# A two-layer LRU, attention and pooling trunk: the scheduler's order of the engine queues taken from its other simulated machine

## The chip, the cores and the metric

One core of a Trainium2 chip runs the kernel. The metric is the device time of one execution in microseconds, the median of the runs shown; less is better.

## The reference

The model has two layers over 2048 rows of 1024 features, and a final norm. Every layer makes 18 column groups of `z` from the normed input, runs three branches on them and projects their gated results back:

```python
for l in range(DEPTH):
    h = rms_norm(x, norm_g[l])
    z = h @ w_in[l]
    za, ga, cq, ckv, kr, gb, zc, gc = jnp.split(z, offsets, axis=-1)
    xa = causal_depthwise_conv(za, conv_w[l], conv_b[l])
    ya = rg_lru(xa, w_rg[l], b_rg[l], w_ig[l], b_ig[l], lru_lambda[l]) * jax.nn.silu(ga)
    yb = mla(cq, ckv, kr, q_norm_g[l], w_uq[l], kv_norm_g[l], w_ukv[l], cos, sin) * jax.nn.silu(gb)
    yc = multi_scale_pool(zc, w_pool[l], pool_scale[l]) * jax.nn.silu(gc)
    y = jnp.concatenate([ya, yb, yc], axis=-1)
    x = x + y @ w_out[l]
return rms_norm(x, final_norm_g)
```

`mla` norms the latents `cq` (384 wide) and `ckv` (256 wide), makes six heads of queries, keys and values from them, and runs causal attention with a rotary part of 32 in every head.

## The kernel before, in words

Data lie transposed: features on the 128 partitions, rows of the sequence along the free dimension, in four chunks of 512. Every matmul operand is split into a high and a low fp16 half, so that a product takes three passes (high by high, high by low, low by high).

**A layer, stage by stage.** `hstage` loads the eight k-tiles of a chunk (L303), multiplies them by the reciprocal norm (L334, alternately on GpSimd, POOL, and on VectorE, DVE), and writes the high half `hA` or `hB` on ScalarE, ACT (L336), and the low half on DVE (L337). `zweight` and `prep` do the same for weights: load (L216), squares on ACT (L222), their sum by a small matmul `pp` on TensorE, PE (L228), a power-of-two scale on DVE (L185 to L190), the halves (L231 on ACT, L232 on DVE). `zgroup` makes one column group of one chunk from 24 matmuls (L378). What follows a group, such as the LRU (L448 to L486), the pooling or the latents (`latent`, L561 to L583, whose column sums of squares are the `pn` matmuls of L245 behind the halves of L238 and L239), runs on ACT and DVE. `values_of` (L719) makes values, copied to `zw` by ACT (L727) and DVE (L728); `keys` is L708, `query` L736, `q_rope` L750. For a softmax without a running maximum, each unit of four query blocks and two heads first has its row maxima taken (`row_max`: matmuls `pm` L777 with two PSUM banks, maxima L782 and L784 on DVE, a transposing matmul L802, and L806 on ACT into a row of `kq`).

**Attention** runs over 12 units (four chunks by three pairs of heads) and over their blocks of 128 keys: scores (L980 to L984), exponentials on ACT (L985), the low half on DVE (L986), the weighted values (L999, L1004). `finish` divides (L949 to L955), transposes (L961), gates to `y` (L963) and stores it (L400).

**Output projection.** `outproj` loads the eight rows of `y` of a chunk (L1023), scales and splits them to `yb` (L1018 and the scale, L1026 on ACT, L1027 on DVE), multiplies them by the output weights (L1046, 24 matmuls per n), adds the load of the old `x` (L1053, L1054), stores the new `x` (L1055) and sums its squares (L1060, L1061) for the next norm. The last chunk of the last layer goes through `outproj_last` (L1073 to L1111). At the end of layer 1, `layer_start` of layer 2 is started beside the last chunk's projection: its `hstage` for chunks 0 and 1 and its first six weights.

**What sets the order.** All of these are Python generators. `spawn` starts one, `tick` advances those that are due, and `between` fills in pieces between matmuls. So the program has one written order. The tile layer then orders each engine's queue itself: it simulates the instructions on a model of the machine and issues what the model finds ready. Loads and stores are all issued from SyncE's queue (SP). Tiles come from pools with fixed numbers of buffers: `T` has 7, `LT` 17; PSUM has three banks under "mm", two under "ax", and one each under "sm", "po" and "su". An engine's queue runs in the order given; an instruction that waits holds up those behind it.

The context that holds this scheduler is opened in `launch`, at L1325:

Of the kernel before, what the change touches and what calls it, by code (L numbers as in the profile page):

```python
# [1316 lines left out]
def launch(nc, ins, outs):  # L1317
    from contextlib import ExitStack

    a = {}  # L1320
    for k, v in ins.items():
        a[k] = nc.dram_tensor(k, v.shape, F32, kind="ExternalInput").ap()
    for k, s in outs.items():
        a[k] = nc.dram_tensor(k, s, F32, kind="ExternalOutput").ap()
    with tile.TileContext(nc) as tc, ExitStack() as ctx:  # L1325
        body(nc, tc, a, ctx)
    if not nc.is_finalized():
        nc.finalize()
# [9 lines left out]
```

## Time and profile before

| what | value |
|---|---|
| median of 3 runs | 2011.38 us |
| lowest and highest run | 2005.93 and 2012.34 us |
| profiled execution | 2005.98 us |
| its span in the trace | 2004.2 us |
| mean granted TensorE clock, as a share of full speed | 0.982 |
| PE busy | 1897.2 us, 95% |
| DVE busy | 1553.8 us, 78% |
| ACT busy | 1159.9 us, 58% |
| POOL busy | 100.7 us, 5% |
| PE instructions in the trace (weight loads apart) | 12524 |

A span is the time from the first to the last instruction in the trace; the execution's own time has 1.8 us more around it. Engine rows overlap, so busy times don't add up to the span. A line number names the line of the kernel that issued an instruction, and `out<-in` its tiles. In the windows and the timeline, times count from the start of the span. A bracket at a row's end gives the idle time of the engine before the row and the instruction that ended it.

### The profile page before, as it was taken

How to read it: one execution, taken by the hardware profiler on the slowest of the kernel's cores; microseconds unless marked ns; L12 is line 12 of the kernel's file. 1: busy time of each engine (PE TensorE's matmuls, PEld its weight loads, DVE VectorE, ACT ScalarE, POOL GpSimd, SP SyncE). 2: the span in 40 equal slices, each digit the busy share in tenths (PEclk: the TensorE clock that was granted, in tenths of full speed). 3: DMA queues.
4: the chain of work that ended last, by engine and by line, in shares of the span. 5: the costliest groups of instructions: out<-in, count | busy, mean ns of one | idle time of the engine just before them, and what ended most of it. 6: DMA issues, size and time to landing. Idle time of an engine off the chain costs nothing. (4 is left out here: it accounts for less than half of the span.)

```text
span 2004.2 us, 33235 instructions
## 1 busy us (share of the span) xinstructions
PE 1897.2 (95%) x12524; PEld 993.1 (50%) x12524; DVE 1553.8 (78%) x3438; ACT 1159.9 (58%) x2042; POOL 100.7 (5%) x70
## 2 busy tenths in 40 slices
PE   7889999899999999999889999999999999999997
PEld 3334444444455555555344444444445555555556
DVE  7987788767788788785868568777587977978756
ACT  7677877644455464464446678775444644545533
POOL 1210000011000000000211000001010000000000
PEclk8999999999999999999899999999999999999999
DMA  5221222203453131122742113212134522322353
GB/s 181 91 73 57 90 74 93 80 28 79 99 172 118 44 91 43 43 70 60 244 146 85 48 58 99 87 61 87 48 83 119 189 64 69 112 64 69 117 163 132
DMA packets 117553, 186.94 MB, mean 93 GB/s; under 512 B 13072, under 2 KB 45968, under 8 KB 117392
## 3 DMA queue, kind: packets, MB, share of 16 engines
q1 hardware_dynamic: 117392, 184.82, 30.0%
q8 instruction: 98, 1.61, 0.4%
q14 instruction: 63, 0.52, 0.1%
HBM read 113.99 MB, written 55.05 MB: 84 GB/s over the span
## 5 line engine op out<-in xcount | busy, mean ns | idle before, releaser
L378 PEld LDWEIGHTS <-zw 128*128 128x128 f16 x3456 | 336.8, 100 | 419.9 <-issue 41.7
L985 ACT ACTIVATE p<-sps,tiny,sig 128x512 f32<-128x512 f32 x480 | 321.3, 710 | 320.8 <-PE sps L982 178.1
L378 PE MATMUL zps<-hA,zw 128*128 128x512 f16 x1728 | 392.3, 384 | 8.0 <-ACT hA L336 4.8
L378 PE MATMUL zps<-hB,zw 128*128 128x512 f16 x1728 | 384.1, 379 | 5.1 <-DVE hB L337 3.3
L1046 PE MATMUL ops<-yb,wo 128*128 128x512 f16 x1344 | 338.0, 384 | 10.8 <-DVE yb L1027 5.7
L986 DVE TENSOR_TENSOR pl<-p 128x1024 f16<-128x1024 f32 x240 | 254.2, 1060 | 102.9 <-ACT p L985 79.0
L782 DVE TENSOR_REDUCE mx<-pm 128x1 f32<-128x512 f32 x288 | 193.0, 683 | 29.7 <-PE pm L777 29.1
L1046 PEld LDWEIGHTS <-wo 128*128 128x128 f16 x1344 | 127.3, 98 | 153.1 <-issue 25.6
L980 PE MATMUL sps<-kq 97*128 97x512 f16 x480 | 167.1, 348 | 0.6 <-ACT p L985 0.6
L981 PE MATMUL sps<-kq 96*128 96x512 f16 x480 | 166.7, 347 | 0.0
L982 PE MATMUL sps<-kq 96*128 96x512 f16 x480 | 165.7, 345 | 0.0
L777 PE MATMUL pm<-kq 96*128 96x512 f16 (+2 forms) x480 | 146.8, 347 | 3.6 <-ACT kq L806 1.4
L999 PE MATMUL av<-zw,p 128*128 128x129 f16 (+1 forms) x1632 | 140.6, 216 | 5.9 <-DVE o L953 5.8
L999 PEld LDWEIGHTS <-p 128*128 128x128 bf16 x1632 | 108.5, 98 | 35.4 <-DVE o L953 5.9
L784 DVE CUSTOM_DVE_ANT_0 pm<-pm,mkq 128x128 f32<-128x128 f32 x192 | 93.2, 494 | 9.8 <-PE pm L777 9.2
L999 PE MATMUL av<-zw,pl 128*128 128x65 f16 x1632 | 94.7, 195 | 1.5 <-DVE pl L986 1.4
L222 ACT ACTIVATE junk<-raw 128x512 bf16<-128x512 f32 (+3 forms) x126 | 75.1, 596 | 16.7 <-DMA raw<-win 13.4
L999 PEld LDWEIGHTS <-pl 128*128 128x128 f16 x1632 | 76.4, 98 | 10.1 <-DVE pl L986 5.4
L334 POOL TENSOR_TENSOR xk<-xk,rb 128x512 f32<-128x512 f32 x28 | 46.2, 1682 | 602.7 <-DVE of L1042 458.4
L982 PEld LDWEIGHTS <-kq 96*128 96x128 f16 x480 | 46.9, 98 | 45.1 <-issue 1.7
L980 PEld LDWEIGHTS <-kq 97*128 97x128 f16 x480 | 46.6, 97 | 44.2 <-issue 4.5
L981 PEld LDWEIGHTS <-kq 96*128 96x128 f16 x480 | 47.2, 98 | 42.3 <-issue 4.1
(301 smaller groups left out, 2848.6 us busy)
## 6 DMA issues: line engine op xcount, KB each, us to landing
raw<-win SPq DMA_DIRECT2D x72, 256.0 KB, 3.5
yr<-y SPq DMA_DIRECT2D x64, 256.0 KB, 4.2
x<-xr SPq DMA_DIRECT2D x56, 256.0 KB, 2.5
xk<-x SPq DMA_DIRECT2D x56, 256.0 KB, 4.8
sg<-sg SPq DMA_DIRECT2D x48, 256.0 KB, 3.6
kq<-pq SPq DMA_DIRECT2D x96, 128.0 KB, 2.4
raw<-wout SPq DMA_DIRECT2D x32, 256.0 KB, 3.6
wo<-wp SPq DMA_DIRECT2D x32, 256.0 KB, 2.7
```

The source lines that it names most:

```text
L222: nc.scalar.activation(junk[:, 0 : kp * n], raw[:, 0 : kp * n], AF.Square, accum_out=ssq[:, i : i + 1])
L378: nc.tensor.matmul(ps[:], w[:, i, k, :], st["h"](j, k, c), start=n == 0, stop=n == 3 * KD - 1)
L777: nc.tensor.matmul(pm[:, 0:n], t[0:96, h, 2, q0 : q0 + 128], t[0:96, h, 0, s * C : s * C + n], start=True, stop=True)
L782: nc.vector.tensor_reduce(m, pm[:], AX.X, ALU.max)
L784: nc.vector.tensor_tensor_reduce(out=pm[:, 0:n], in0=pm[:, 0:n], in1=mkq[:, C - n : C], op0=ALU.add, op1=ALU.max, scale=1.0, scalar=-3.0e3 ...
L980: nc.tensor.matmul(ps[:, o:C], t[0:97, h, 0, ks], t[0:97, h, 2, qs], start=True, stop=False)
L981: nc.tensor.matmul(ps[:, o:C], t[0:96, h, 0, ks], t[0:96, h, 3, qs], start=False, stop=False)
L982: nc.tensor.matmul(ps[:, o:C], t[0:96, h, 1, ks], t[0:96, h, 2, qs], start=False, stop=not diag)
L985: nc.scalar.activation(pw_[:, h, o:C], ps[:, o:C], AF.Exp, scale=sig[:, 4:5], bias=tiny[:, 1:2])
L986: nc.vector.tensor_tensor(pl[:, :, o:C], pw_[:, :, o:C], ph[:, :, o:C], ALU.subtract)
L999: nc.tensor.matmul(acc[h][:, c - 64 * lo : c + 65], w, v[:, 64 - 64 * lo : QB], start=first and n == 0 and j == 0, stop=end and n == 1 and ...
L1046: nc.tensor.matmul(ps[:], w[:, i, k, :], yb[:, j, k, :], start=m == 0, stop=m == 3 * KD - 1)
```

## The change

The context is opened with one more argument. It makes the tile layer's scheduler run the other of its two simulated machines, and the queues are ordered by what that one finds ready:

```diff
@@ -1322,7 +1322,7 @@
         a[k] = nc.dram_tensor(k, v.shape, F32, kind="ExternalInput").ap()
     for k, s in outs.items():
         a[k] = nc.dram_tensor(k, s, F32, kind="ExternalOutput").ap()
-    with tile.TileContext(nc) as tc, ExitStack() as ctx:
+    with tile.TileContext(nc, schedule_with_timeline_sim=True) as tc, ExitStack() as ctx:
         body(nc, tc, a, ctx)
     if not nc.is_finalized():
         nc.finalize()
```

The instructions stay the same: 12446 matmuls by the program's count, 801 DMAs, and every ACT and DVE operation. What moves is their place in the queue of their engine: 8894 of PE's 12451 places hold another instruction than before, 2788 of DVE's, 1174 of ACT's, 304 of SP's; POOL's order is the same. Semaphore waits are set anew for the new order.

**First place: ACT at the start.** `raw` are loaded weights, `lsa` squares of the first chunk, `zw_72` the weights' halves, and `hA` the halves of the first normed chunk. Before:

```order
L319 ACTIVATE lsa<-lsa 128x512 x2
L222 ACTIVATE junk,ssq<-raw 128x512 x2
L231 ACTIVATE zw_72<-raw,zsc 128x512 x2
L222 ACTIVATE junk,ssq<-raw 128x512 x2
L319 ACTIVATE lsa<-lsa 128x512
L231 ACTIVATE zw_72<-raw,zsc 128x512
L336 ACTIVATE hA<-xk,gs 128x512 x7
```

Now:

```order
L319 ACTIVATE lsa<-lsa 128x512 x4
L222 ACTIVATE junk,ssq<-raw 128x512 x3
L231 ACTIVATE zw_72<-raw,zsc 128x512 x2
L222 ACTIVATE junk,ssq<-raw 128x512
L231 ACTIVATE zw_72<-raw,zsc 128x512 x2
L222 ACTIVATE junk,ssq<-raw 128x512 x3
L132 ACTIVATE sp<-sp 128x6
L133 ACTIVATE sp<-sp 128x6
L222 ACTIVATE junk,ssq<-raw 128x512
L336 ACTIVATE hA<-xk,gs 128x512 x3
```

More squares and halves of weights, and the two small gate rows, stand ahead of the first `hA`.

**Second place: ACT in the value stage of layer 1.** `krt` is the rotary key, `ckh` the normed latent, `vps` the PSUM tile of a value group, which L727 and then L728 read. Before:

```order
L615 ACTIVATE krt<-kr 128x512
L222 ACTIVATE junk,ssq<-raw 128x384
L222 ACTIVATE junk,ssq<-raw 128x192
L561 ACTIVATE raw<-zps,zsc 128x512
L222 ACTIVATE junk,ssq<-raw 128x384
L564 ACTIVATE acc<-raw 128x512
L582 ACTIVATE ckh<-raw 128x512
L222 ACTIVATE junk,ssq<-raw 128x192
L582 ACTIVATE ckh<-raw 128x512
L222 ACTIVATE junk,ssq<-raw 128x384
L727 ACTIVATE zw_72<-vps 128x6x64
```

Now:

```order
L561 ACTIVATE raw<-zps,zsc 128x512
L564 ACTIVATE acc<-raw 128x512
L615 ACTIVATE krt<-kr 128x512
L727 ACTIVATE zw_72<-vps 128x6x64
L582 ACTIVATE ckh<-raw 128x512
L222 ACTIVATE junk,ssq<-raw 128x384
L582 ACTIVATE ckh<-raw 128x512
L222 ACTIVATE junk,ssq<-raw 128x192
L727 ACTIVATE zw_72<-vps 128x6x64
```

The copy of the value group stands ahead of the two L582 where it stood behind them.

**Third place: DVE and SP at the boundary of the layers.** `o` and `y` are the last attention unit's, `yb_10560` the halves of the last chunk's `y`, `xr` the new `x`; `rb`, `xk` and `hA` belong to the `hstage` of layer 2. DVE before:

```order
L955 TENSOR_TENSOR o<-o,r 128x512
L963 SCALAR_TENSOR_TENSOR y<-pt,gbf,sg 128x512
L185 TENSOR_REDUCE ysc<-pp 128x1
L187 TENSOR_SCALAR ysc<-ysc 128x1
L188 TENSOR_SCALAR hb<-ysc 128x1
L189 TENSOR_SCALAR hb<-ysc 128x1
L190 TENSOR_SCALAR ysc<-hb 128x2
L1042 TENSOR_TENSOR of<-wosc,ysc 128x1
L1027 SCALAR_TENSOR_TENSOR yb_10560<-yr,ysc,yb_10560 128x512 x4
L1054 SCALAR_TENSOR_TENSOR xr<-ops,of,xr 128x512
L271 STREAM_TRANSPOSE rb<-ry 128x512
```

DVE now (between the last row here and the first L1027 stand the four rows L187 to L190, two L1042, one L1054, one L271, four L334 and seven L337):

```order
L955 TENSOR_TENSOR o<-o,r 128x512
L271 STREAM_TRANSPOSE rb<-ry 128x512
L334 TENSOR_TENSOR xk<-xk,rb 128x512 x3
L337 SCALAR_TENSOR_TENSOR hA<-xk,gs,hA 128x512 x2
L963 SCALAR_TENSOR_TENSOR y<-pt,gbf,sg 128x512
L337 SCALAR_TENSOR_TENSOR hA<-xk,gs,hA 128x512
L334 TENSOR_TENSOR xk<-xk,rb 128x512
L337 SCALAR_TENSOR_TENSOR hA<-xk,gs,hA 128x512 x3
L185 TENSOR_REDUCE ysc<-pp 128x1
```

SP at the same place, before:

```order
L946 DMA sg<-sg_95 128x512
L303 DMA xk<-x_101 128x512 x4
L1023 DMA yr<-y_93 128x512
L400 DMA y_93<-y 128x512
L1023 DMA yr<-y_93 128x512 x3
L1053 DMA xr<-xT 128x512
```

SP now:

```order
L946 DMA sg<-sg_95 128x512
L303 DMA xk<-x_101 128x512 x14
L1023 DMA yr<-y_93 128x512 x4
L400 DMA y_93<-y 128x512
L1053 DMA xr<-xT 128x512
```

Work of the next layer's first chunks now stands ahead of the last unit's `y` and of the halves `yb` made from it.

## Rows read from the trace of the kernel before

**Rows 1.** The page: span, busy time of two engines, one group of matmuls

```profile
span 2004.2 us, 33235 instructions
...
PE 1897.2 (95%) x12524; PEld 993.1 (50%) x12524; DVE 1553.8 (78%) x3438; ACT 1159.9 (58%) x2042; POOL 100.7 (5%) x70
...
L378 PE MATMUL zps<-hA,zw 128*128 128x512 f16 x1728 | 392.3, 384 | 8.0 <-ACT hA L336 4.8
```

**Rows 2.** Windows by stage (window, its length, busy us of each engine)

```profile
core 0: us, PE busy (x) PEld busy (x) DVE busy (x) ACT busy (x) POOL busy (x), PEclk, DMA share, GB/s
0.00:50.00 50.00, 36.08 (x136) 15.89 (x137) 39.97 (x144) 36.18 (x73) 6.94 (x8) 0.83 0.54 181
50.00:150.00 100.00, 85.47 (x378) 37.48 (x377) 91.41 (x174) 68.96 (x109) 19.38 (x12) 1.00 0.25 81
...
240.00:420.00 180.00, 167.51 (x851) 79.19 (x849) 143.53 (x364) 129.76 (x244) 13.72 (x13) 0.99 0.26 81
420.00:945.00 525.00, 512.31 (x4098) 284.55 (x4096) 407.47 (x852) 264.74 (x462) 10.84 (x4) 0.99 0.27 77
945.00:1050.00 105.00, 90.29 (x415) 40.87 (x414) 77.11 (x177) 49.08 (x93) 17.82 (x11) 0.92 0.60 190
1050.00:1215.00 165.00, 165.00 (x772) 78.15 (x771) 118.01 (x231) 118.32 (x189) 9.09 (x6) 1.00 0.22 74
1215.00:1400.00 185.00, 174.79 (x875) 82.69 (x874) 146.29 (x365) 133.92 (x251) 12.04 (x13) 0.97 0.25 79
1400.00:1925.00 525.00, 511.61 (x4103) 283.52 (x4103) 418.60 (x870) 265.36 (x462) 10.83 (x4) 0.99 0.31 93
1925.00:2004.00 79.00, 64.13 (x490) 47.42 (x488) 46.72 (x122) 24.64 (x51) 0.00 (x0) 0.95 0.49 163
```

**Rows 3.** Waits of PE (waiting, waited for: us in total, times, longest)

```profile
PE pn L245 <- ACT sqh L238: 16.2, 8, 6.1
...
PE vps L719 <- DVE zw L728: 7.7, 2, 4.0
...
PE ops L1046 <- DVE yb L1027: 5.7, 5, 2.9
```

**Rows 4.** Timeline of ACT and PE, start (start, duration, instruction, idle before)

```profile
19.59 0.61 ACT L222 ACTIVATE junk<-raw 128x512 bf16<-128x512 f32 x1
...
20.33 0.63 ACT L222 ACTIVATE junk<-raw 128x512 bf16<-128x512 f32 x1
...
24.25 1.33 ACT L336 ACTIVATE hA<-xk,gs 128x512 f16<-128x512 f32 x2 [1.07 <-POOL xk L334]
...
25.02 1.01 PE L378 MATMUL zps<-hA,zw 128*128 128x512 f16 x2 [3.33 <-ACT hA L336]
```

**Rows 5.** Timeline of ACT and PE in the value stage of layer 1

```profile
413.71 0.63 ACT L582 ACTIVATE ckh<-raw 128x512 f16<-128x512 f32 x1 [2.88 <-DVE raw L581]
...
415.99 0.47 ACT L727 ACTIVATE zw<-vps 128x384 f16<-128x384 f32 x1
...
417.11 2.08 PE L719 MATMUL vps<-wv,ckh 128*128 128x384 f16 x6 [3.98 <-DVE zw L728]
```

**Rows 6.** Timeline of SP, DVE and PE at the boundary of the layers

```profile
949.28 1.75 SPq L303 DMA_DIRECT2D xk<-x  x4
...
952.17 0.75 DVE L963 SCALAR_TENSOR_TENSOR y<-pt,gbf,sg 128x512 f32<-128x512 f32 x1 [0.81 <-PE pt L961]
...
957.77 0.75 DVE L1027 SCALAR_TENSOR_TENSOR yb<-yr,ysc,yb 128x512 f16<-128x512 f32 x1 [2.62 <-ACT yb L1026]
...
963.36 0.69 DVE L334 TENSOR_TENSOR xk<-xk,rb 128x512 f32<-128x512 f32 x1
...
967.33 4.09 DVE L337 SCALAR_TENSOR_TENSOR hA<-xk,gs,hA 128x512 f16<-128x512 f32 x3
...
972.14 3.43 PE L1046 MATMUL ops<-yb,wo 128*128 128x512 f16 x9 [2.87 <-DVE yb L1027]
```

**Rows 7.** Timeline of PE in the projections of layer 1, 160 to 175 us

```profile
159.96 15.27 PE L378 MATMUL zps<-hA,zw 128*128 128x512 f16 x70
```

## The prediction

> **What bounds the kernel now.** I read the page first. TensorE (PE) is busy for 1897.2 of 2004.2 us, VectorE (DVE) for 1553.8 [rows 1]. No engine loses work by the change, so what it can win is PE's idle time, 2004.2 - 1897.2 = 107 us, and what the lower granted clock costs: the mean clock of the profiled execution is 0.982, so 2004 x 0.018 = 36 us of full-speed columns were not granted, part of them while PE idled anyway.
>
> The table of windows then says in which stage the idle time lies [rows 2]: 13.9 us in the start (0 to 50), 14.5 from 50 to 150, 12.5 from 240 to 420 (latents, values, keys and queries of layer 1), 12.7 in the attention of layer 1 (420 to 945), 14.7 at the boundary of the layers (945 to 1050), 10.2 from 1215 to 1400 (latents and values of layer 2), 13.4 in the attention of layer 2, 14.9 in the end. In the two long attention stages PE is busy 97.5% of the time, so there is little to win there and, by length, most to lose. From 50 to 150 DVE is busy 91.41 of 100 us: there it is DVE's own work that paces PE.
>
> The list of PE's waits last: the largest group is the sums of squares of a row chunk (L245) that wait for ACT's L238, 16.2 us in 8 times; two value groups (L719) wait 7.7 us for L728; the output projection (L1046) waits 5.7 us for its input halves (L1027) [rows 3]. These are short chains over ACT and DVE, in which an instruction that is ready stands behind one that is not. Another order can repair that; it can also make more of it.
>
> **The change, part by part.** Every sum is against the profiled execution, 2005.98 us; the median of the runs is 2011.38, 5.4 us above it. I take the differences as they are and set them against the median. A measurement of this kernel tells a difference from none at about 0.3%, 6 us.
>
> *Start: +4 us.* The first hA of L336 decides when PE begins its projections: PE's first L378 starts at 25.02 us after 3.33 us of idle, right behind the hA that starts at 24.25 [rows 4]. In the new ACT order four more L222, one more L231, one L319 and the two L132/L133 stand ahead of that hA. Two L222 in a row start 0.74 us apart (19.59 and 20.33, with the short read of the sum behind each). Taking the same 0.74 for the L231 and the L319, which have the same 128x512 shape, and 0.2 for each of the two small ones, this is 6 x 0.74 + 0.4 = 4.8 us. Some of it lies in the 1.07 us that ACT waits before this very hA: about 4. Bounds: 2, if all these weights are ready early, and 6, if the extra L222s wait for their loads, which need freed T buffers. The weights prepared early come back as earlier matmuls; that gain is in the next part.
>
> *50 to 150: -5 us.* Weights are prepared further ahead. PE's idle time is 14.5 us, but DVE keeps all its work, and its own idle time is only 8.6 us: that is the most that order can give back, nothing is the least. I take a little over half.
>
> *Latents and values of layer 1: -9 us.* A group that shows how: two L582 stand in ACT's queue ahead of L727, and the first waits 2.88 us for DVE's L581. The L727, whose value group had long left PE, runs at 415.99; PE's next value group waits 3.98 us for the bank [rows 5]. In the new order L727 stands ahead of both L582, and its DVE partner L728 moves ahead by 18 positions, so this wait goes. One L238 of this stage moves forward 8 places, and the L245 on PE that reads it stands 85 matmuls later, behind work that is ready; its wait, one of the eight of [rows 3], goes too. Of the stage's 12.5 us I take 9; at least 4 (the one value wait), at most 12.
>
> *The same stage of layer 2: -7 us* of 10.2, by the same moves (the second of the two waits in the row of L719 is here); 4 to 10.
>
> *Boundary: +5 us.* SP now issues fourteen next-layer loads (L303) where it issued four, then the loads of the last rows of y; four of these took 1.75 us to issue, so the loads of yr stand ten further back, 4.4 us. On DVE, before: L963 (y) at 952.17, the first half yb (L1027) at 957.77. Now one L271, three L334 and two L337 of the next layer stand ahead of L963, with 0.69 for an L334 and as much for the L271 and each L337 (all 128x512) 6 x 0.69 = 4.1 us alone, and 6 x 1.36 = 8.2 at the pace of three L337 that take 4.09 us. Behind y eleven more L337 and five L334 stand ahead of the first L1027 (16 x 0.69 = 11 us). It waited 2.62 us for ACT before, so part of this fits in [rows 6]. I expect yb and the xr of L1054 some 12 to 14 us later than now, and PE waits for them, since ops of the last chunk need all yb. Against that, part of today's 14.7 us of idle time goes: the 2.87 us before 972.14 becomes part of the new wait, and the next layer's hA and hB are there earlier, so its projections start without waiting, and the wait of 6.1 us (the longest in the row of L245) shrinks only a little, because the chain of load, L1054 and store behind it stays. 13 for the new wait, less 8 of the old idle time (a little over half), is +5; bounds -3 (PE finds projections for the whole wait) and +13 (none of the old idle time goes).
>
> *Attention: -3 us over both layers.* The matmuls of the row maxima (L777) move back by 74 matmul positions in the mean, L802 by 63, L961 by 47, L1018 by 64, the av groups (L999) forward by 12. Of today's 26.1 us of idle time I take half as gained: -13. But L777's banks are two, and DVE's max (L782) moves back with it: where a later L777 releases a later L782, the query rows (kq) that a unit needs come later. I allow one such wait in each of the 24 units (12 in a layer), as long as two matmuls of 0.216 us [rows 7]: +10. Bounds: -20 and +10.
>
> *End: +1.5 us* (-1 to +4): eight loads of L1073 now stand ahead of one xr load instead of five (three times 0.44 us), and L1018 of the last chunk comes 26 matmuls later.
>
> *Clock: -3 us* (-6 to +4). The windows with long waits have 0.92 (boundary) and 0.97 (1215 to 1400), those without 1.00 [rows 2]. 185 x 0.03 = 5.6 us of columns in the latter; half of it comes back if its waits go. The boundary's stays.
>
> Sum: 4 - 5 - 9 - 7 + 5 - 3 + 1.5 - 3 = -16.5 us, so 1989.5 for a profiled execution and **1995 us** against the median.
>
> **The rivals.**
> *Slower, by the boundary.* The order puts work of the next layer before the y and yb that PE waits for. If the wait is the full 13 us with none of today's idle time gone, the clock falls for longer (at the boundary's 0.92, 8 us of 105 are lost already; I take 5 more), the start costs 6, the later L777 costs the attention its 10 with nothing won, and the end 1.5, this is +35.5, against the -5 - 9 - 7 = -21 that stay: +14.5, 2026 us; with the attention's cost halved 2021. For it: PE's row of 2.87 us shows that it already waits for yb. Against: the projections are then ready for PE to fill in. With the other terms as I sum them, it turns the sign from a new wait at the boundary of about 30 us (13 + 16.5), or from 1.1 us of new waiting in every attention unit (26.5 / 24).
>
> *No change.* DVE is at 78% and the order doesn't shorten its work; waits that go from PE come back two steps later as the chain of another tile. The three groups named above are 29.6 of the 107 us; the rest is spread over many pairs, so there is much to take their place. The gains of 21 halved, attention and clock at nothing, the costs as summed: 4 - 2.5 - 4.5 - 3.5 + 5 + 1.5 = 0, 2011 us, give or take 6.
>
> *A larger gain.* PE's delays between matmuls are partly invisible. Seventy L378 in a row take 15.27 us [rows 7], that is 0.216 us each, while the page counts 0.384 us for one [rows 1]; so a delay of up to 0.17 us between two never shows as idle time. If the later L777 and L961 also remove such delays, some 10 us in the attention stages (an estimate, two matmuls of 0.216 us in each unit) come on top of the 20 of the bound: -16.5 - 17 - 10 = -43.5, 1968 us; with half of the 27 1981. The Trainium skill (Perfetto Trace Analysis, Identifying the Most-Contended Engine) says that matmul busy time is no good measure of how near a kernel is to its limit, and that the busy share of weight loads is better. This trace agrees as to the measure: 0.216 against 0.384. The same page (Optimization Strategy, under Identifying Performance Opportunities) says that stages bound by different engines may gain from being interleaved. The new order does that at the boundary; by the rule the 14.7 us there would go, where I sum +5. This case's row speaks against it: DVE is already busy for 77.11 of those 105 us, and is what PE waits for. It is part of this rival: -16.5 - 19.7 = -36, 1975 us.
>
> **How the numbers follow.** My own case, 6 to 25 us faster, has 0.43, the larger gain 0.15, no change 0.19, slower 0.23. Faster is then 0.58, same 0.19, slower 0.23. The range reaches to the middle of the larger gain, 1974, and, since the costs at the boundary and in the attention are the worst known terms, to 2020 in the slower rival; about 1 in 10 lies outside on either side. The likeliest case alone is 1986 to 2005.
>
> **What would show it.** In the profile after: PE's first L378 at about 29 us; no wait of L719 for L728 above 1 us in either layer, and L245's group well under 16.2; from 240 to 420 under 5 us of idle time; at the boundary L963 at least 4 us later behind L955 and one wait of PE for L1027 or L1054 of 10 us or more; many small new waits of L980 or L777 in the attention, of under 1 us. I am wrong if the boundary's window loses under 10 or over 30 us, if the waits at L719 are still there, or if the attention stages change by more than 20 us either way.

## The result, and the profile after

The changed kernel takes 2055.53 us (2052.70 to 2061.30 in 4 runs), the kernel before 2008.66 us beside it (2004.63 to 2012.34). The ratio is 1.0234, with a 95% interval from 1.0215 to 1.0254: 2.3% slower, where 0.8% faster was forecast. The profiled execution took 2052.70 us.

Page of the changed kernel, span and busy times:

```profile
span 2050.9 us, 33223 instructions
...
PE 1904.2 (93%) x12524; PEld 1000.2 (49%) x12524; DVE 1548.0 (75%) x3438; ACT 1162.7 (57%) x2042; POOL 95.6 (5%) x70
```

PE idles for 147 us where it idled for 107 [rows 1], and its mean clock is 0.965 where it was 0.982. PE itself is busy for 7.0 us more, ACT for 2.8 us more, DVE and POOL for less. To see where this lies, the trace after is cut where PE has issued as many matmuls as at the ends of the windows before (the counts behind PE's time are nearly those of [rows 2]). Windows of the changed kernel (window, its length, busy us of each engine):

```profile
core 0: us, PE busy (x) PEld busy (x) DVE busy (x) ACT busy (x) POOL busy (x), PEclk, DMA share, GB/s
0.00:54.10 54.10, 36.04 (x137) 16.12 (x138) 44.94 (x168) 38.28 (x76) 6.85 (x8) 0.81 0.55 183
54.10:146.70 92.60, 85.22 (x380) 38.37 (x379) 83.83 (x138) 65.72 (x105) 19.36 (x12) 0.98 0.22 78
146.70:236.90 90.20, 90.20 (x426) 43.45 (x425) 66.96 (x156) 69.36 (x112) 0.00 (x0) 1.00 0.23 74
236.90:402.50 165.60, 165.37 (x852) 79.36 (x851) 136.18 (x350) 128.37 (x237) 10.03 (x11) 1.00 0.28 88
402.50:956.20 553.70, 516.86 (x4101) 287.10 (x4099) 413.38 (x868) 269.93 (x473) 12.45 (x7) 0.97 0.25 73
956.20:1069.70 113.50, 87.60 (x419) 41.13 (x416) 77.06 (x163) 51.02 (x98) 18.49 (x12) 0.89 0.52 167
1069.70:1240.70 171.00, 167.24 (x773) 78.72 (x772) 117.62 (x244) 117.54 (x185) 6.35 (x4) 0.99 0.23 78
1240.70:1411.20 170.50, 170.38 (x876) 81.38 (x875) 140.22 (x361) 131.00 (x246) 11.25 (x13) 1.00 0.27 85
1411.20:1973.70 562.50, 524.03 (x4106) 288.03 (x4105) 422.07 (x875) 267.67 (x465) 10.84 (x4) 0.95 0.29 88
1973.70:2050.90 77.20, 61.30 (x473) 46.54 (x471) 45.74 (x122) 23.80 (x51) 0.00 (x0) 0.97 0.49 159
```

Stage by stage, the difference to the windows before is +4.1 (start), -7.4, +0.2, -14.4 (latents and values of layer 1), **+28.7 (attention of layer 1)**, +8.5 (boundary), +6.0, -14.5 (latents and values of layer 2), **+37.5 (attention of layer 2)** and -1.8 us (end). The two stages before the attentions are now almost without idle time, 0.2 and 0.1 us where 12.5 and 10.2 were. All of the loss, and more, is in the attentions, 66 us. Of these, 49 us are PE's idle time (26.1 us in both attentions before, 75.3 now) and 17 us its longer busy time (512.3 to 516.9 us and 511.6 to 524.0), at a granted clock of 0.97 and 0.95 where it was 0.99.

Waits of PE in the changed kernel (waiting, waited for: us in total, times, longest):

```profile
PE ops L1046 <- DVE xr L1054: 21.7, 13, 12.0
PE pr L802 <- DVE nm L797: 15.6, 13, 1.9
PE av L999 <- DVE o L953: 13.9, 2, 7.1
PE pm L777 <- ACT kq L806: 10.7, 19, 3.1
PE pm L777 <- DVE mx L782: 8.7, 30, 0.5
...
PE pp L1018 <- ACT junk L401: 6.7, 1, 6.7
PE pm L777 <- DVE mx L784: 5.7, 13, 2.3
PE pn L245 <- ACT sqh L238: 5.3, 1, 5.3
```

Rows of L802 and L777 in the kernel before:

```profile
PE pr L802 <- DVE nm L797: 2.5, 3, 1.6
...
PE pm L777 <- ACT kq L806: 1.4, 2, 1.1
...
PE pm L777 <- DVE mx L782: 0.9, 3, 0.5
```

L245's group fell from 16.2 to 5.3 us and L719's wait for L728 is gone [rows 3]. What has grown most is the row maxima's chain: its four rows (L802 for L797, L777 for L806, L782 and L784) come to 40.7 us, 1.7 us for each of the 24 units, where the kernel before has 4.8. They are many short waits: none of L802's is over 1.9 us, and of L777's 62 all but two are under 0.7 us. L777 waits for L806 since the tile that L806 reads, `pr`, takes its bank from the same two ("ax") as `pm`. New are also the two waits of the boundary (12.0 and 6.7) and two of about 7 us of L999 for L953, one in each attention.

What a unit's beginning looks like now is shown by the eleventh unit of layer 1. Timeline of PE in the changed kernel, from the last row maxima (L777) of the unit to its first score (L980):

```profile
852.45 0.38 PE L777 MATMUL pm<-kq 96*128 96x512 f16 x1
852.67 0.60 PE L1046 MATMUL ops<-yb,wo 128*128 128x512 f16 x2
853.11 0.38 PE L777 MATMUL pm<-kq 96*128 96x512 f16 x1
855.31 0.61 PE L802 MATMUL pr<-idb,nm 128*1 128x128 bf16 x8 [1.82 <-DVE nm L797]
856.37 0.38 PE L777 MATMUL pm<-kq 96*128 96x512 f16 x1 [0.46 <-ACT kq L806]
856.59 0.38 PE L980 MATMUL sps<-kq 97*128 97x512 f16 x1
```

The same unit in the kernel before:

```profile
842.33 0.60 PE L777 MATMUL pm<-kq 96*128 96x512 f16 x2
842.89 1.67 PE L1046 MATMUL ops<-yb,wo 128*128 128x512 f16 x7
...
845.78 0.61 PE L802 MATMUL pr<-idb,nm 128*1 128x128 bf16 x8 [0.23 <-DVE nm L797]
846.32 0.82 PE L1046 MATMUL ops<-yb,wo 128*128 128x512 f16 x3
...
847.85 0.38 PE L980 MATMUL sps<-kq 97*128 97x512 f16 x1
```

The chain is the same: maxima on PE, DVE's maximum, L797, L802 on PE, the copy to `kq` by L806, the first score. Before, PE has matmuls of the projection, of scores and of values between its links: 27 between the last L777 and L802, 7 between L802 and L980. After, there are none and one, and PE waits for what DVE and ACT do: of the 3.5 us from 853.11 to 856.59, which have ten matmuls in them, it idles for 2.28, where it idled for 0.23 between the same two links before. In 18 of the 24 units at most one matmul is left between L802 and the unit's first score, where before none had fewer than two. None is left between the last L777 and L802 in eight units, the last three of layer 1 among them; before, these three had 19, 27 and 25, and no unit fewer than 8. In the first units, too, the row of `kq` comes later against its use: from the end of L806 to the unit's first score it was 34.4, 5.5, 0.7, 61.7, 5.1, 13.0, 3.3 and 3.3 us in the first eight units of layer 1, and is 4.6 in the first, 37.4 in the fourth, 3.3 in the fifth and nothing in the others.

Boundary, timeline of DVE, SP and PE in the changed kernel:

```profile
961.78 8.79 SPq L303 DMA_DIRECT2D xk<-x  x14
...
973.39 0.74 DVE L963 SCALAR_TENSOR_TENSOR y<-pt,gbf,sg 128x512 f32<-128x512 f32 x1
...
974.93 0.59 PE L1018 MATMUL pp<-ssy,on 128*128 128x8 f32 x2 [6.71 <-ACT junk L401]
...
987.49 12.70 PE L1046 MATMUL ops<-yb,wo 128*128 128x512 f16 x50 [11.97 <-DVE xr L1054]
...
990.09 2.72 DVE L1027 SCALAR_TENSOR_TENSOR yb<-yr,ysc,yb 128x512 f16<-128x512 f32 x4
```

SP's fourteen loads take 8.79 us to issue, y comes 9.5 us behind the end of L955 (963.85), and PE waits 18.7 us in two pieces.

### The profile page after: what moved, and what is told of

Read it like the earlier page. It is cut to its first block, busy times and chain, and to the rows that moved or that the text cites. A ratio compares the mean times of both kernels' runs of the same rounds, so it can differ in the third digit from the quotient of the medians.

```text
span 2050.9 us, 33223 instructions
## 1 busy us (share of the span) xinstructions
PE 1904.2 (93%) x12524; PEld 1000.2 (49%) x12524; DVE 1548.0 (75%) x3438; ACT 1162.7 (57%) x2042; POOL 95.6 (5%) x70
## 4 chain that ended last, share of the span: by engine, by line
PE 70%; DVE 16%; DMA 6%; ACT 5%; issue 2%; SPq 1%; POOL 0%; DVEq 0%; ACTq 0%
PE zps L378 25%; PE ops L1046 11%; PE av L999 6%; PE sps L980 4%; PE sps L981 4%; PE sps L982 4%; PE pm L777 3%; PE ops L1085 2%; PE qps L736 2%; DVE xk L334 2%; PE kps L708 1%; DMA xr<-xT 1%; DVE mx L782 1%; PE qrp L750 1%; DMA raw<-win 1%
## 5 line engine op out<-in xcount | busy, mean ns | idle before, releaser
L378 PEld LDWEIGHTS <-zw 128*128 128x128 f16 x3456 | 336.0, 99 | 416.9 <-issue 36.0
L985 ACT ACTIVATE p<-sps,tiny,sig 128x512 f32<-128x512 f32 x480 | 328.6, 711 | 249.7 <-PE sps L984 112.9
L378 PE MATMUL zps<-hA,zw 128*128 128x512 f16 x1728 | 390.7, 383 | 4.1 <-ACT hA L336 2.1
L378 PE MATMUL zps<-hB,zw 128*128 128x512 f16 x1728 | 384.1, 380 | 5.8 <-DVE sg L676 4.0
L1046 PE MATMUL ops<-yb,wo 128*128 128x512 f16 x1344 | 325.3, 384 | 25.4 <-DVE xr L1054 21.7
L782 DVE TENSOR_REDUCE mx<-pm 128x1 f32<-128x512 f32 x288 | 193.2, 684 | 68.3 <-PE pm L777 61.6
L777 PE MATMUL pm<-kq 96*128 96x512 f16 (+2 forms) x480 | 163.0, 358 | 26.5 <-ACT kq L806 10.7
L999 PE MATMUL av<-zw,p 128*128 128x129 f16 (+1 forms) x1632 | 163.7, 216 | 13.9 <-DVE o L953 13.9
L980 PE MATMUL sps<-kq 97*128 97x512 f16 x480 | 172.7, 360 | 0.7 <-ACT kq L806 0.7
L981 PE MATMUL sps<-kq 96*128 96x512 f16 x480 | 171.9, 358 | 0.0
L982 PE MATMUL sps<-kq 96*128 96x512 f16 x480 | 170.4, 355 | 0.0
L999 PEld LDWEIGHTS <-p 128*128 128x128 bf16 x1632 | 114.4, 99 | 51.4 <-DVE o L953 15.5
L784 DVE CUSTOM_DVE_ANT_0 pm<-pm,mkq 128x128 f32<-128x128 f32 x192 | 93.7, 494 | 51.7 <-PE pm L777 49.6
L999 PE MATMUL av<-zw,pl 128*128 128x65 f16 x1632 | 104.8, 194 | 1.3 <-DVE pl L986 1.3
L999 PEld LDWEIGHTS <-pl 128*128 128x128 f16 x1632 | 84.8, 98 | 23.8 <-DVE pl L986 2.4
L222 ACT ACTIVATE junk<-raw 128x512 bf16<-128x512 f32 (+3 forms) x126 | 75.3, 598 | 31.4 <-DMA raw<-win 24.4
L806 ACT ACTIVATE kq<-pr 1x512 f16<-1x512 f32 x48 | 25.9, 581 | 97.1 <-PE pr L802 96.9
L334 POOL TENSOR_TENSOR xk<-xk,rb 128x512 f32<-128x512 f32 x28 | 44.1, 1600 | 640.3 <-DMA xk<-x 469.3
L777 PEld LDWEIGHTS <-kq 96*128 96x128 f16 x480 | 46.0, 98 | 52.6 <-issue 30.5
L1060 ACT ACTIVATE sq<-xr 128x512 f32<-128x512 f32 x49 | 30.7, 626 | 71.8 <-DVE xr L1054 67.9
```

What stands on the lines that cost most here:

```text
L334: eng.tensor_tensor(xs[k], xs[k], rb, ALU.mult)
L378: nc.tensor.matmul(ps[:], w[:, i, k, :], st["h"](j, k, c), start=n == 0, stop=n == 3 * KD - 1)
L777: nc.tensor.matmul(pm[:, 0:n], t[0:96, h, 2, q0 : q0 + 128], t[0:96, h, 0, s * C : s * C + n], start=True, stop=True)
L782: nc.vector.tensor_reduce(m, pm[:], AX.X, ALU.max)
L784: nc.vector.tensor_tensor_reduce(out=pm[:, 0:n], in0=pm[:, 0:n], in1=mkq[:, C - n : C], op0=ALU.add, op1=ALU.max, scale=1.0, scalar=-3.0e3 ...
L980: nc.tensor.matmul(ps[:, o:C], t[0:97, h, 0, ks], t[0:97, h, 2, qs], start=True, stop=False)
```

## The experiments

All kernels of the experiments are built in one way: behind the program's body, edges are added that fix the order of two instructions in the queue of one engine and add no semaphore wait of their own. The machine named orders what the edges leave open, so other instructions can move too. The "front" of a layer is all of its stages ahead of its attention. Shortened, with the lists of pairs told by what they hold:

```diff
+def pin(nc, tc):
+    seen = {i.name: i for i in nc.cur_bb.bb.instructions}
+    for first, then in PAIRS:
+        tc.add_manual_dep(
+            seen[then], first,
+            mybir.DependencyInfo(mybir.DependencyClass.NoSync, mybir.DependencyReason.DATA), reason="pin",
+        )
...
         body(nc, tc, a, ctx)
+        pin(nc, tc)
```

What differs is the list of pairs and the machine that orders the rest.

**1. Is the front's gain real?** Every queue is fixed as a whole: the new order up to 470 us of the new trace, the old one behind it.

```diff
+PAIRS = neighbours(new_order[start < 470] + old_order[the rest])  # each engine
```

> The queues of all engines have the new order up to 470 us of the new trace (before the first row maximum, L777), and the old order for all that is left. Theory A (the attention's new order costs time by itself, the front's new order wins it): the 19 to 25 us that the new trace is ahead at that point stay to the end, so 1984 to 1990 us against 2008. Rival B (the front's gain is only borrowed: the attention that begins earlier finds loads and latents not there and gives it back whatever its order): 2005 to 2010 us.

Measured: 1995.04 us against 2007.87, ratio 0.9934 (0.9915 to 0.9954). The part up to the attention is 404.5 us long where it was 421.2 with the same number of matmuls; the attention then takes 528.2 us, 3.6 more than before. Most of the gain stays, a part is given back: theory A, with a smaller number than I gave.

**2. Both fronts.** The same, and the new order also from 1100 us of the old trace to 1482 us of the new one.

> As the run before, and the new order also for layer 2 from 1100 us of the old trace to 1482 us of the new one, just ahead of the row maxima; old order in both attentions, at the boundary and in the end. Theory A: another 15 to 18 us less than with the front of layer 1 alone, about 1968 to 1973 us. Rival B: 2005 to 2010 us.

Measured: 1986.45 us against 2007.87, ratio 0.9888 (0.9867 to 0.9909). Layer 2's front adds 8.6 us to the gain, not 15. The sign of theory A holds, its size doesn't. In the two traces the stage ahead of layer 2's attention did shrink by 15 us, from 185.3 to 170.4 us; other stages grew, the second attention most, by 5.7. Why they did isn't shown.

**3. The attention of layer 1 alone.** The old order up to 487 us, the new one up to 955 us of the new trace, the old one for the rest.

> Old order up to 487 us of the old trace, new order for the attention of layer 1 up to 955 us of the new trace, old order again for the rest. Theory A: the attention of layer 1 alone costs 30 to 36 us, so 2038 to 2044 us. Rival B: the order is no worse by itself when the attention doesn't begin earlier, 2005 to 2015 us.

Measured: 2040.82 us against 2007.87, ratio 1.0164 (1.0139 to 1.0189): 33 us slower. The attention needs no early beginning and no other stage of the new order to be slow.

**4. Row maxima back, in the new order.** 672 pairs on PE: each L777 and L802 ahead of the PE instruction ahead of which it stood before; the new machine orders the rest.

```diff
+PAIRS = [(x, next_other_on_PE(x, old_order)) for x in L777 + L802]
```

> The new order, but every row maximum's matmul (L777) and transposing matmul (L802), 672 in all, must stand ahead of that PE instruction ahead of which it stood before; all else is ordered anew by the new machine. Theory A1 (the loss in the attention is the late row maxima: PE has run out of scores when the row of kq of the next unit is still on its way): most of the 78 us of both attentions come back, 1965 to 1990 us. Rival A2 (the loss comes from the orders of DVE and SP: o and y late behind the rotary chain, wo loads ahead of the rotary tables): 2035 to 2055 us, and both PE waits of about 7 us for L953 are still there.

Measured: 2015.19 us against 2007.87, ratio 1.0040 (1.0026 to 1.0055). 40 of the 47 us are back. Windows of this kernel, attention of layer 1 and of layer 2:

```profile
402.70:934.50 531.80, 509.06 (x4099) 283.83 (x4098) 415.47 (x869) 269.42 (x471) 12.26 (x6) 0.99 0.26 76
...
1390.00:1934.80 544.80, 519.43 (x4106) 285.71 (x4105) 423.01 (x875) 267.69 (x465) 10.84 (x4) 0.97 0.30 90
```

They are 7 and 20 us longer than before, not 29 and 37. That is more than A2 allows and less than A1 asked for: 40 of 66 us come back. The waits of L999 for L953 have 2.5 us for the longest where they had 7.1. Two matmuls or more stand between L802 and the first score in every unit again. But a row maximum is held to its old neighbour, and that one has moved too: L777 stands 19 matmul positions behind its old place in the mean, where the new order has 74.

**5. Row maxima late, in the old order.** The reverse, on the kernel before: the same 672 matmuls stand behind the PE instruction behind which the new order puts them, and the old machine orders all else.

```diff
+PAIRS = [(last_other_on_PE(x, new_order), x) for x in L777 + L802]
...
     with tile.TileContext(nc) as tc, ExitStack() as ctx:
```

> The kernel before, with the old machine's order, but each of the 672 matmuls L777 and L802 must stand behind that PE instruction behind which the new order puts it. The rest is the old machine's. Theory A1 (late row maxima alone cost the attention its time): 2035 to 2050 us. Rival A2 (late row maxima do harm only together with the new order's other queues): 2005 to 2018 us.

Measured: 2074.49 us against 2009.23, ratio 1.0322 (1.0303 to 1.0341), 65 us slower; more than I expected, since I had left the second layer's share too small. Windows of this kernel, both attentions:

```profile
422.20:975.60 553.40, 520.06 (x4099) 287.08 (x4098) 410.08 (x852) 263.90 (x461) 10.84 (x4) 0.98 0.25 73
...
1432.90:1992.80 559.90, 525.20 (x4105) 287.29 (x4104) 423.16 (x862) 263.75 (x459) 10.84 (x4) 0.96 0.30 88
```

Waits of PE in this kernel:

```profile
PE pr L802 <- DVE nm L797: 14.4, 13, 1.8
...
PE pm L777 <- ACT kq L806: 8.4, 18, 0.7
```

553.4 and 559.9 us: the new kernel's 553.7 and 562.5, with the same waits of the chain (15.6 and 10.7 us there) and at most one matmul between L802 and the first score in 17 units. Only the row maxima were put late; around them the old machine moved other work of its own (3427 of PE's other 11774 places hold another matmul than before). So the late place of the row maxima is enough to make the loss of both attentions. That nothing else of the new order costs time there is not shown; runs 4 and 7 speak against it.

**6. The boundary alone.** Every queue fixed: old order up to 940 us, new up to 1062 us of the new trace, old again.

> The old order up to 940 us of the old trace, the new one up to 1062 us of the new trace (the end of layer 1 and the start of layer 2), the old one for the rest. Theory A (next-layer work ahead of y and yb on DVE and SP costs about 19 us of PE's time in two waits and saves about 8 of today's): 2012 to 2018 us, with PE waits near 7 us for L401 and near 12 us for L1054. Rival (the waits come from the attention that ends late, not from the boundary's own order): 2004 to 2010 us, without them.

Measured: 2016.23 us against 2009.23, ratio 1.0032 (1.0019 to 1.0045): +7.0 us. Waits of PE in this kernel:

```profile
PE ops L1046 <- DVE xr L1054: 15.8, 9, 12.0
...
PE pp L1018 <- ACT junk L401: 7.1, 1, 7.1
```

Both waits are the boundary's own.

**7. PE's queue old, all others new.** Only PE's 12446 matmuls are fixed.

```diff
+PAIRS = neighbours(old_order["PE"])
```

> PE's whole queue has the old order; ACT, DVE, SP and POOL are ordered by the new machine around it. Theory A: the fronts' gain is partly in the other queues (ACT's L727, L238), so a little of it stays; the attention is as before; the boundary's waits stay: 2000 to 2015 us. Rival A2 (the other queues make the attention slow): 2025 to 2050 us.

Measured: 2066.54 us against 2009.23, ratio 1.0288 (1.0271 to 1.0305). A miss: worse than either whole order. The gains of the fronts are gone (the stage before the first attention is as long as before), and PE now waits in its old place for DVE's new one. Waits of PE in this kernel:

```profile
PE ops L1046 <- DVE yb L1027: 15.2, 9, 3.6
PE pm L777 <- DVE mx L782: 13.3, 18, 2.3
```

The attentions are 539.0 and 550.6 us here, 14 and 26 more than before, so the other queues in their new order cost the attentions time even with PE's row maxima in their old places. It doesn't refute run 5, where the old machine ordered them; it shows that this mix is worse than either whole order.

**8. Both fronts, old start.** Run 2 with the old order up to 62 us.

> As the kernel with the two new fronts and old attentions (1986.45 us), but with the old order up to 62 us of the old trace. If the new start costs 4 us by itself: 1981 to 1984 us. If the weights that it prepares early are what shortens 50 to 150 us: 1986 to 1992 us.

Measured: 1981.48 us against 2009.23, ratio 0.9861 (0.9840 to 0.9881), the fastest of all. It is 5 us less than run 2, but the two intervals overlap (run 2's begins at 0.9867), so a cost of the new start by itself is not shown. Nor do the traces show one: the stage ahead of the first attention begins at 237.9 us here, and with the new start at 236.9 (the changed kernel) to about 241 us (run 2). Windows of this kernel, the stage ahead of the first attention, and both attentions:

```profile
237.90:403.90 166.00, 165.39 (x852) 79.37 (x851) 136.51 (x353) 128.60 (x237) 10.60 (x11) 1.00 0.27 88
403.90:931.50 527.60, 512.43 (x4100) 284.55 (x4098) 413.00 (x868) 267.02 (x472) 12.44 (x7) 0.99 0.26 76
...
1374.10:1899.10 525.00, 508.52 (x4103) 281.19 (x4102) 420.11 (x875) 265.47 (x465) 10.84 (x4) 1.00 0.31 94
```

**9. The copies of values ahead, in the old order.** 32 L727 on ACT and 32 L728 on DVE.

> The kernel before with the old machine's order, but each of the 32 L727 on ACT and the 32 L728 on DVE must stand ahead of the instruction ahead of which the new order puts it. If the two waits of 4.0 and 3.7 us of L719 for L728 were one link of the front's gain: 408 to 430 us and 1385 to 1410 us lose about 4 us each, the waits are under 1 us, and the time is 1999 to 2006 us. If another wait takes their place in the same stage: 2005 to 2010 us.

Measured: 1991.15 us against 2006.77, ratio 0.9918 (0.9888 to 0.9949). Better than I expected: these 64 places, with what the old machine moves around them, give 0.5 to 1.1% where run 8 gives 1.4%. The trace is of the slowest of the four executions, 1999.00 us; in it the two stages ahead of the attentions are 177.3 and 177.9 us long where they were 180 and 185. No wait of L719 for L728 is left; its largest is this:

```profile
PE vps L719 <- DVE pq L700: 1.0, 2, 0.8
```

**10. The sums of squares late, in the old order.** 106 matmuls L245 and L228 on PE.

> The kernel before with the old machine's order, but each of the 106 matmuls of the sums of squares (L245 and L228) must stand behind that PE instruction behind which the new order puts it. If PE's early place for them was the other link of the front's gain: the waits of L245 for L238 (16.2 us) and of L228 for L222 (11.0 us) shrink by 8 to 12 us in sum, 1997 to 2004 us. If what reads the sums becomes late in its turn: 2005 to 2012 us.

Measured: 2006.14 us against 2006.77, ratio 0.9998 (0.9985 to 1.0012). The front of layer 1 is 174.1 us long where it was 180.3, that of layer 2 178.1 where it was 185.1; but the attentions take 527.6 and 530.0 us, and the projections between 1051 and 1221 us take 4 more. The two waits shrank by 16 us in sum, more than asked (16.2 to 6.0 and 11.0 to 5.1), and yet the time is the same: the gain is given back. L245 and L228 also serve the output projection and its weights; that their late place there is what gives it back is my reading, not shown.

**11. The whole chain back.** Run 4 with L782, L784, L793, L797 on DVE and L806 on ACT fixed in the same way, 1242 pairs in all.

> The new order, and as in the run that took 2015.19 us each L777 and L802 stands ahead of that PE instruction ahead of which it stood before; now the same holds for the rest of the chain too, L782, L784, L793 and L797 on DVE (522 in all) and L806 on ACT (48). If what was left of the loss in the attentions (7 us in layer 1, 21 in layer 2) is DVE's late half of the same chain: attentions of 524 to 530 us each, and 1988 to 2000 us in all. If it is something else in the new order (av, ops and loads around it): attentions as with PE's half alone, and 2010 to 2018 us.

Measured: 2028.48 us against 2009.30, ratio 1.0090 (1.0071 to 1.0109): worse than run 4, a miss on both counts. The attentions are 540.4 and 549.5 us, where run 4 has 531.8 and 544.8. Waits of PE in this kernel:

```profile
PE av L999 <- DVE o L953: 9.1, 4, 3.9
...
PE av L999 <- DVE pl L986: 5.2, 10, 1.1
```

With the chain pushed ahead on DVE, `o` and `pl` come late. So what run 4 left, 7 and 20 us in the attentions, stays open: it isn't simply DVE's half of the chain.

## Why the prediction was wrong

The forecast was 1995 us and faster; it is 2055.5 and slower, outside the range. The step that failed is one: *"Attention: -3 us over both layers"*, with bounds of -20 and +10. It measured +28.7 and +37.5. Of its two halves, the -13 for idle time gained did not come: PE's idle time there rose from 26.1 to 75.3 us. The +10 for the chain of the row maxima, 0.43 us for a unit, was mis-sized: its waits came to 40.7 us where they had been 4.8, 1.5 us more for a unit, and 17 us more is PE's longer busy time at the lower clock, for which the forecast had 4 at the most (the clock's upper bound). The other terms hold in sign but for the end and the clock, and the stages outside the attentions became 19 us shorter in sum, more than the 13.5 that I had forecast for all but the attentions:

- Start: +4 forecast, +4.1 measured; PE's first L378 is at 28.44 us (about 29 forecast).
- 50 to 150: -5 forecast, -7.4 measured, near the bound that DVE's idle time set (-8.6).
- Latents and values: -9 and -7 forecast, -14.4 and -14.5 measured. Nearly all idle time went (12.3 and 10.1 us) where I took 9 and 7 of it, and the clock came back with it, which I had counted apart and small: 0.99 to 1.00 over 180 us is 1.8 us, 0.97 to 1.00 over 185 us is 5.6.
- Boundary: +5 forecast, +8.5 in the trace and +7.0 alone (run 6). The mechanism was as told; the new wait is 18.7 us, not 13. Of the old idle time 7.5 us went where I took 8, and PE is busy for 2.7 us less in this window.
- 1050 to 1215: nothing forecast, +6.0 measured. PE idles for 3.8 us where it had no idle time, 3.2 of them in one wait of L463 for DVE's L436.
- End: +1.5 forecast, -1.8 measured.
- Clock: -3 forecast; the mean fell from 0.982 to 0.965, most of it in the attentions (0.99 to 0.97 and 0.95), as part of the same loss. I had tied the clock to windows with long waits; in the attentions it also fell where all waits were short.

How the failed step came about: I had the right move, the row maxima 74 positions later in the mean, and the right chain, L777 to `kq`. I then priced it by a small wait, two matmuls in each of 24 units. A mean shift doesn't say what is left between an instruction and the one that needs it. That stood in PE's new queue to be read: behind the last L777 of a late unit comes L802, and behind that the first score, with nothing or one matmul between. Where that is so, a unit pays for most of the chain: 2.28 us of idle time in 3.5 us from L777 to L980 in the eleventh unit. The mean over the 24 units, 1.5 us more than before, is past the 1.1 us at which I had put the turn of the sign, and I had held a wait of that size to be unlikely with no row for it. Runs 3 and 5 show the place of the loss and that the late row maxima are enough to make it; what makes the 27 us that are left with the row maxima back (run 4) stays open.

Of the rivals, the slower one named the boundary as the cause and 2026 us; its sign was right, its place and size were not. The larger gain's 1981 us was reached by run 8, but through the fronts, with the old order in both attentions; the mechanism which that rival named, shorter delays within the attentions, was not seen.

The Trainium skill (Perfetto Trace Analysis, Optimization Strategy) says that stages bound by different engines may gain from being interleaved. I had written that this case's row speaks against it at the boundary, and the measurement agrees: run 6 costs 7.0 us, and in the changed kernel PE waits there for DVE, which is busy for 77.06 of 113.5 us.

## What to carry to other kernels

When a scheduler moves thousands of instructions, don't sum the shifts: for each chain that leaves an engine and comes back to it, count in the new queue what work of that engine is left between the links. Where it is none, the price is most of the chain, once for each time it runs (2.28 of 3.5 us in the unit shown). And a scheduler's two orders can be joined by stage: here the new one was better ahead of the attentions and the old one in them, and the joined order (run 8) was 1.4% faster than the kernel before, while the one mix by engine that was tried (run 7) was slower than either.

## What the runs showed that I had not expected

PE's clock fell in stretches without any long wait. Window of the changed kernel, within the attention of layer 1:

```profile
900.00:920.00 20.00, 16.98 (x82) 7.86 (x81) 12.65 (x29) 5.32 (x13) 0.00 (x0) 0.83 0.26 69
```

Timeline of PE in it:

```profile
911.42 0.38 PE L777 MATMUL pm<-kq 96*128 96x512 f16 x1 [0.22 <-DVE mx L782]
913.11 1.01 PE L802 MATMUL pr<-idb,nm 128*1 128x128 bf16 x8 [1.31 <-DVE nm L797]
...
914.75 0.63 PE L981 MATMUL sps<-kq 96*128 96x512 f16 x1
```

The longest wait in it is that of L802 at 913 us, 1.31 us, behind five waits of L777 of 0.15 to 0.28 us each; PE idles for 3.0 us in all and is granted 0.83, a mixture of its two levels, 2.4 and 1.2 GHz: an L981 takes 0.63 us behind it where it takes 0.38 at the full clock. Before, the window of the same unit had 1.00. Not every fall is of this kind; one in each attention stands around the 7 us wait of L999. So here the short waits cost twice, by their idle time and by slower matmuls behind them, and run 5, with the row maxima late and no such wait of L999, has 0.98 and 0.96 too. In layer 2's attention of the changed kernel it is 38.5 us of idle time (13.4 before) and 562.5 x 0.05 = 28 us that were not granted (525 x 0.01 = 5 before), in part at the same time.
